# A decoder block on one core: modulation steps in pairs, work moved to ScalarE, and 18 matmuls of ones in the opening

## The chip, the cores and the metric

The kernel runs on 1 core of one Trainium2 chip. The metric is device time in microseconds, from the start to the end of one launch; less is better. The time before is the median of three runs. The profile shows one execution of the same program.

## The reference

One layer of a hybrid decoder block, 512 tokens of 1024 channels, all in float32:

```python
mod = silu(c) @ w_ada + b_ada            # c: (1, 1024), w_ada: (1024, 6 * 1024)
shift1, scale1, gate1, shift2, scale2, gate2 = split(mod, 6)
h = rms_norm(x, g_pre_mix) * (1 + scale1) + shift1
z = h @ w_in                             # GLU 2048 | q latent 384 | kv latent 256 | rotary key 64 | gates 2048
u = causal_depthwise_conv(ua * sigmoid(ub), 31 taps)
y_a = silu(layer_norm(u)) @ w_conv_out
y_b = mla_attention(...) @ w_attn_out    # 8 heads, rotary parts with cos and sin of the positions
x = x + gate1 * rms_norm((sigmoid(g_a) * y_a + sigmoid(g_b) * y_b) @ w_out, g_post_mix)
h = rms_norm(x, g_pre_mlp) * (1 + scale2) + shift2
x = x + gate2 * rms_norm(relu(h @ w_mlp_in) ** 2 @ w_mlp_out, g_post_mlp)
```

## The kernel before, in words

**Products.** A float32 product is made of three matmuls of a faster 32-bit type (`mm3`): each operand is split in a high part (a cast, on ScalarE) and a low part (the difference, on VectorE). So every weight block costs ScalarE one cast and VectorE one subtraction before TensorE can use it. TensorE transposes and the few products with ones remain in plain float32; one such product is recorded as two matmuls.

**Order of the work.** The function `emit` does not issue instructions. It records them, each with an engine, a cost and its dependences, in a `Planner`. The planner then simulates the five engines: TensorE takes of the ready operations the one with the lowest rank (its place in the program, less a `boost`), the others the one that is due first (`dead`, worked back from TensorE's schedule, less a `hurry`). It repeats this for up to `PASSES` = 14 allocations of the buffers, keeps the plan with the shortest simulated length and issues its order. Each engine's queue is thus a fixed order; on the chip semaphores alone delay it. `Planner.cost` holds the prices of instructions; the cost of a DMA's issue on SP is 375 ns there, a DMA's duration is worked out in `record`, and at most `DEPTH` = 8 loads are in flight on SP's queue. `plan.slack` adds a delay to the end of a POOL instruction in the simulation, `plan.after` a dependence on one operation. Both exist in the kernel before.

**The opening.** SP loads c (as `c8`, 8 rows of 128), x in four tiles, bias rows, and the first blocks of `w_ada`. TensorE transposes `c8` into a bank of PSUM (`bc`), VectorE and ScalarE form silu(c) in `cT`. x's tiles are normalised and transposed, 32 transposes in all, into `xnT`. Then the modulation of the first sublayer is formed for each block `k` of 128 channels (k = 0 to 7):

- `ada_load(ks, step)` loads the columns of shift and scale for the blocks in `ks`, in pieces of `step` rows of blocks; `KGRP` gives the groups, before `(1,)` to `(7,)`. One block's row in memory is 128 floats, 512 bytes.
- `ada_sums` multiplies by c: for k = 0 and 1 with TensorE (8 products of a column of `cT` by 128 x 256, 16 records each), for the others with VectorE (one `tensor_scalar` and seven `scalar_tensor_tensor` over 256 columns).
- `to_columns` sums over partitions with a product by ones, four small products for each k, and VectorE adds the bias and forms shift and scale (`mod[:, 0]`, `mod[:, 1]`).
- `first_products` forms h for block k from these (two activations and a difference) and multiplies seven blocks of `w_in` with it, 21 matmuls of 512 columns for each k, accumulating in seven banks of PSUM.

**After it** come the rest of the input projection, the latents, the rotary tables (`rp`: two Sin activations on ScalarE after the range reduction), attention by heads, the gates, the layer norm, the output products and the MLP. The convolution's 31 taps run on VectorE for eight channel blocks, spread over the products by `pump`: the first tap is a `tensor_scalar` that writes `cacc` from `upad`, the other 30 are `scalar_tensor_tensor`. They must be done before the layer norm, whose reciprocal root is a power on POOL (`lns`), followed by products of ones with a scaled identity that spread it over the partitions.

Nearly all instructions go through `record` and `issue`, so the profile gives them line 433; they are told apart by engine, tiles and shapes.

Of the kernel before, what the change touches and what calls it, by code (L numbers as in the profile page):

```python
# [17 lines left out]
P = 128  # L18
T = 512
# [36 lines left out]
ADAS = (1, 1, 0, 4)  # L56
KGRP = ((1,), (2,), (3,), (4,), (5,), (6,), (7,))
HL, SQ = 5e3, False
EXCL = True
LAG, AJ = 3000.0, 1  # L60
KOUT, VK = False, (0,)
ADD, LATE5 = 2.6, 1
HX, HA, HG, HC = 1.2e5, 1e5, 3e3, 1.1e5

# [114 lines left out]
class Planner:  # L179
# [68 lines left out]
    def cost(self, eng, fn, outs, ins, k):  # L248

        n = max(self.free_size(o) for o in (ins if fn == "reduce_sum" else outs))  # L250
        if fn == "dma_start":
            return (1200.0, 3000.0) if eng == "pool" else (375.0, 2000.0)
        psum = any(r.tensor.name.startswith("psum") for r in ins + outs)
# [7 lines left out]
        if eng == "act":  # L261
            t = 0.833 * n + (51 if psum else 93) + 93 * scalars + (900 if AF.Sin in self.args else 0)
            if fn == "activation" and any(isinstance(v, bass.AP) for v in outs[1:]):
                t += 93
            return t, 150.0
# [10 lines left out]
    def record(self, eng, fn, a, k):  # L276
# [19 lines left out]
        if fn == "dma_start":  # L296
            b = 4
            for _, c in outs[0].ap:
                b *= c
            n = min(self.run(outs[0]), self.run(ins[0]), 4096)  # L300
            o.dma = b * (6.0 + 0.040 * n) / (16 * n) * (ADD if eng == "pool" else 1)
        deps = set()
# [135 lines left out]
def tile_hybrid_block(  # L438
# [25 lines left out]
    def tile_of(shape, dtype, name):  # L464
        if name not in tiles:
            tiles[name] = const.tile(shape, dtype, name=name)
        return tiles[name]

    hD = [tc.dram_tile([P, KD * T], F32, name=f"h_spill{i}") for i in range(2)]
    yD = [tc.dram_tile([P, D], F32, name=f"y_spill{t}") for t in range(NT)]  # L470
    ident = const.tile([P, P], F32, name="ident")
    make_identity(nc, ident)
    ones = const.tile([P, P], F32, name="ones")
    nc.gpsimd.memset(ones, 1.0)
    nhalf = const.tile([P, 8], F32, name="nhalf")
# [11 lines left out]
    def emit(past, replay):  # L487
# [128 lines left out]
        plan.hurry = 0.0  # L616

        bc = pb.alloc()
        pe.transpose(pb.v(bc)[:, 0:8], c8, ident[:8, :8])
        cT = tile_of([P, 8], F32, "cT")  # L620
        tmp8 = tile_of([P, 8], F32, "tmp8")
# [20 lines left out]
        b1p = tile_of([P, 16], F32, "b1p")  # L642
        pool.tensor_scalar(b1p[:, 0:8], col("bada", 8, 8), 1.0, None, ALU.add)
        pool.tensor_scalar(b1p[:, 8:16], col("bada", 32, 8), 1.0, None, ALU.add)

# [36 lines left out]
        def to_columns(srcs, ks):  # L682

            for s in range(2):
                for i, k in enumerate(ks):
                    for src, lp in srcs:
                        pe.matmul(pb.v(bg)[:, s * KD + k:s * KD + k + 1], lhsT=src[:, s, i * P:(i + 1) * P],
                                  rhs=ones[0:lp, 0:1], start=src is srcs[0][0], stop=src is srcs[-1][0])
            ksl = slice(ks[0], ks[-1] + 1)
            dve.tensor_tensor(mod[:, 0, ksl], pb.v(bg)[:, ksl], col("bada", ks[0], len(ks)), ALU.add)  # L690
            for k in ks:
                dve.scalar_tensor_tensor(mod[:, 1, k:k + 1], pb.v(bg)[:, KD + k:KD + k + 1], b1p[:, k:k + 1], col("gpm", k),
                                         op0=ALU.add, op1=ALU.mult)

# [60 lines left out]

        for ks in KGRP:
            plan.hurry = HA - 1e4 * ks[0]
            ada = ada_load(ks, 1 if ks[0] == 1 and PE1 else KD // 2)
            ada_end = len(plan.ops) - 1
            plan.hurry -= 5e3  # L760
            wbs = [g1_load(k) for k in ks]
            plan.hurry = HG
            plan.boost = 1000
            if ks[0] == 1:
                plan.hurry = H1
                ada_sums(ks, ada, PE1, CH1)
            else:
                ada_sums(ks, ada)
            for k, wb in zip(ks, wbs):
                first_products(k, wb)  # L770
# [42 lines left out]
        rp = tile_of([P, 4, NT, NR], F32, "rp")  # L813
        ang, nn_, cosk, sink = (rp[:, i] for i in range(4))
        pool.tensor_tensor(ang, posT[:, :, None].broadcast_to([P, NT, NR]), invf[:, None, :].broadcast_to([P, NT, NR]), ALU.mult)
# [13 lines left out]
        dve.tensor_scalar(ngf, ngf, -1.0, float(np.float32(np.pi / 2)), ALU.mult, ALU.add)  # L829
        act.activation(sink, ang, AF.Sin)  # L830
        act.activation(cosk, nn_, AF.Sin)

# [18 lines left out]
        def conv_ops():  # L851
            for g in CONV_DVE:
                for kk in range(TAPS):
                    for ct in g:
                        if kk == 0:
                            cacc[ct] = fa.alloc(T)
                            dve.tensor_scalar(fa.v(cacc[ct]), fa.v(upad[ct])[:, 0:T], cw[:, ct, 0:1], col("cb", ct),
                                              ALU.mult, ALU.add)
                        else:
# [443 lines left out]
        def layer_norm():  # L1303
# [12 lines left out]
            dve.tensor_tensor(nb, ns, dm, ALU.subtract)  # L1316
            dve.tensor_tensor(va, va, rs, ALU.subtract)
            pool.tensor_tensor(rs, va, nhalf[:, :NT], ALU.pow)
            dve.tensor_tensor(nb, nb, rs, ALU.mult)

# [543 lines left out]
```

## Time and profile before

| | before |
|---|---|
| median of three runs | 808.56 us (807.07 to 809.38) |
| the profiled execution | 807.76 us, span 805.6 us, mean granted clock 0.998 |
| busy: TensorE / weight loads | 789.3 us (98%) / 687.6 us (85%) |
| busy: VectorE / ScalarE / POOL | 735.8 us (91%) / 476.6 us (59%) / 59.6 us (7%) |
| DMA | 130.99 MB, mean 163 GB/s |

Times in the profile count from the first instruction (span). The 2.2 us between span and time lie outside of it. An engine's busy share says where it works, not whether anyone waits for it; matmuls are pipelined, so a matmul's own duration (392 ns for 512 columns) is longer than the distance between two of them.

### The profile page before, as it was taken

Reading aid. Unit: us, or ns where it says so; the run is one execution under the profiler, and the core shown is the slowest. Engines: PE = TensorE matmul, PEld = TensorE weight load, DVE = VectorE, ACT = ScalarE, POOL = GpSimd, SP = SyncE. Lnnn points to the kernel's source line nnn. Section 1 sums busy time; section 2 is a strip of 40 time slices with the busy share of each in tenths; the row PEclk is TensorE's granted clock in tenths of the full one; section 3 lists DMA queues with packets and bytes.
Section 4 is the critical chain, followed back from the end, with each engine's and each line's share of the span. In section 5 each row is a group of like instructions: output and inputs, shape, how many; then the busy total and the mean of one; then the engine's idle time right before and its main releaser. Section 6 shows DMA issues by size and latency. Waiting matters only on the chain.

```text
span 805.6 us, 12015 instructions
## 1 busy us (share of the span) xinstructions
PE 789.3 (98%) x4450; PEld 687.6 (85%) x4450; DVE 735.8 (91%) x1052; ACT 476.6 (59%) x790; POOL 59.6 (7%) x121
## 2 busy tenths in 40 slices
PE   6999999999999999999999999999999999999996
PEld 3888988889897888878888889988998899889985
DVE  2899999999999999999898579899989978997998
ACT  5564463375886247238343268777667766777852
POOL 2001010000000000010000010001003300320023
PEclk9999999999999999999999999999999999999999
DMA  8999433010363272143997026149806940895176
GB/s 265 315 266 371 131 116 113 27 54 27 118 197 105 79 224 64 53 157 131 326 364 250 28 93 226 49 131 302 324 28 148 285 143 27 177 270 193 29 160 139
DMA packets 100364, 130.99 MB, mean 163 GB/s; under 512 B 8817, under 2 KB 67538, under 8 KB 100306
## 3 DMA queue, kind: packets, MB, share of 16 engines
q1 hardware_dynamic: 93970, 118.69, 44.7%
q0 software_dynamic: 6336, 11.54, 9.0%
q8 instruction: 35, 0.57, 0.3%
q14 instruction: 23, 0.19, 0.1%
HBM read 109.23 MB, written 20.97 MB: 162 GB/s over the span
## 4 chain that ended last, share of the span: by engine, by line
PE 84%; DVE 11%; issue 2%; ACT 2%; DMA 1%; POOL 0%; SPq 0%; DVEq 0%; ACTq 0%
PE psum L433 84%; DVE f_arena L433 6%; DVE r_arena L433 5%; ACT r_arena L433 1%; DMA rows<-in_b_ada_dram 1%; ACT f_arena L433 1%; DMA r_arena<-h_spill 0%; SPq L433 0%; POOL lns L433 0%; DVEq L1859 0%; POOL stats L433 0%; DVE lns L433 0%; DVE stats L433 0%; DVEq L433 0%; ACTq L433 0%
## 5 line engine op out<-in xcount | busy, mean ns | idle before, releaser
L433 PE MATMUL psum<-r_arena 128*128 128x512 f32 (+3 forms) x4108 | 749.4, 343 | 0.3 <-DVE r_arena L433 0.2
L433 PEld LDWEIGHTS psum<-r_arena 128*128 128x128 f32 x4108 | 647.8, 189 | 86.0 <-DVE r_arena L433 2.0
L433 ACT CAST r_arena<-f_arena 128x1024 fp32r<-128x1024 f32 (+4 forms) x249 | 236.6, 970 | 174.9 <-PE psum L433 115.2
L433 DVE TENSOR_TENSOR r_arena<-f_arena,r_arena 128x1024 fp32r<-128x1024 f32 (+5 forms) x259 | 278.0, 1101 | 26.5 <-ACT r_arena L433 23.7
L433 DVE SCALAR_TENSOR_TENSOR f_arena<-f_arena,cw 128x512 f32<-128x512 f32 x240 | 166.4, 754 | 0.0
L433 DVE TENSOR_TENSOR f_arena<-f_arena 128x1024 f32<-128x1024 f32 (+3 forms) x104 | 110.1, 1072 | 3.7 <-DMA f_arena<-in_w_mlp_in_dram 3.2
L433 ACT COPY f_arena<-psum 128x512 f32<-128x512 f32 (+4 forms) x107 | 57.5, 551 | 34.4 <-PE psum L433 30.4
L433 ACT ACTIVATE f_arena<-f_arena 128x512 f32<-128x512 f32 (+3 forms) x117 | 67.0, 593 | 17.2 <-DVE f_arena L433 16.2
L433 DVE SCALAR_TENSOR_TENSOR f_arena<-f_arena,cT 128x256 f32<-128x256 f32 (+1 forms) x70 | 54.4, 803 | 2.0 <-DMA f_arena<-in_w_ada_dram 1.6
L433 POOL DMA_DIRECT2D y_spill<-f_arena x40 | 34.8, 870 | 263.8 <-ACT f_arena L433 260.6
L433 DVE TENSOR_TENSOR f_arena<-psum,f_arena 128x512 f32<-128x512 f32 (+1 forms) x43 | 28.7, 677 | 12.1 <-PE psum L433 9.3
L433 PE MATMUL psum<-ident,f_arena 128*128 128x128 f32 x234 | 33.0, 280 | 5.2 <-DVE f_arena L433 5.2
L433 ACT ACTIVATE f_arena<-psum 128x512 f32<-128x512 f32 x35 | 20.5, 596 | 28.4 <-PE psum L433 21.2
L433 PEld LDWEIGHTS psum<-ident,f_arena 128*128 128x128 f32 x234 | 27.3, 143 | 11.0 <-DVE f_arena L433 5.5
L433 DVE TENSOR_TENSOR r_arena<-psum,r_arena 128x512 fp32r<-128x512 f32 (+2 forms) x57 | 36.0, 662 | 0.4
L433 ACT CAST r_arena<-psum 128x512 fp32r<-128x512 f32 (+2 forms) x57 | 30.0, 564 | 9.3 <-PE psum L433 8.9
L433 POOL TENSOR_TENSOR stats<-stats,nhalf 128x1 f32<-128x1 f32 (+1 forms) x17 | 12.3, 722 | 169.5 <-ACT stats L433 147.5
L433 ACT ACTIVATE r_arena<-f_arena 128x512 fp32r<-128x512 f32 (+3 forms) x21 | 13.5, 645 | 16.1 <-DVE f_arena L433 13.8
L433 ACT ACTIVATE r_arena<-psum 128x512 fp32r<-128x512 f32 x12 | 7.2, 598 | 24.5 <-PE psum L433 24.5
L433 POOL TENSOR_TENSOR lns<-lns,nhalf 128x4 f32<-128x4 f32 x1 | 2.0, 2046 | 251.4 <-DVE lns L433 251.4
L433 DVE CUSTOM_DVE_ANT_0 f_arena<-psum,mask 128x128 f32<-128x128 f32 (+3 forms) x32 | 15.0, 489 | 0.0
L433 DVE SCALAR_TENSOR_TENSOR f_arena<-f_arena 128x512 f32<-128x512 f32 (+1 forms) x18 | 13.3, 757 | 0.1
(94 smaller groups left out, 211.8 us busy)
## 6 DMA issues: line engine op xcount, KB each, us to landing
f_arena<-in_w_ada_dram SPq DMA_DIRECT2D x32, 512.0 KB, 5.0
f_arena<-in_w_mlp_in_dram SPq DMA_DIRECT2D x32, 512.0 KB, 9.4
f_arena<-in_w_mlp_out_dram SPq DMA_DIRECT2D x32, 512.0 KB, 5.7
f_arena<-in_w_in_dram SPq DMA_DIRECT2D x24, 512.0 KB, 4.4
y_spill<-f_arena POOLq DMA_DIRECT2D x40, 256.0 KB, 6.3
f_arena<-in_w_ada_dram SPq DMA_DIRECT2D x24, 256.0 KB, 5.9
f_arena<-in_x_dram SPq DMA_DIRECT2D x8, 512.0 KB, 7.4
h_spill<-r_arena SPq DMA_DIRECT2D x16, 256.0 KB, 6.6
```

The source lines that it names most:

```text
L433: getattr(self.real[o.eng], o.fn)(*o.a, **o.k)
```

## The change

Modulation blocks 2 to 7 are loaded and summed in pairs, so that a row in memory has 256 floats and VectorE's operations have 512 columns; the pieces loaded are two row blocks instead of four. The two steps that add bias and form scale go from VectorE to ScalarE, with a product b1g formed on POOL ahead of them. The convolution's first tap goes from VectorE to ScalarE. Sine and cosine are one activation over both halves of `rp`, whose order is changed for it. TensorE multiplies `ones` by `ones` three times before the transpose of c and fifteen times after it, into a bank that nothing reads, and `ones` is set ahead of the identity. The planner's numbers for a DMA's issue on SP, a DMA's duration and a Sin change, and the power of the layer norm gets 1100 ns of slack in the simulation. Since the order comes from the simulation, all queues may change their order.

```diff
-KGRP = ((1,), (2,), (3,), (4,), (5,), (6,), (7,))
+KGRP = ((1,), (2, 3), (4, 5), (6, 7))
...
+ISS = 480.0
+SPIN = (3, 15)
...
-            return (1200.0, 3000.0) if eng == "pool" else (375.0, 2000.0)
+            return (1200.0, 3000.0) if eng == "pool" else (ISS, 2000.0)
...
-            t = 0.833 * n + (51 if psum else 93) + 93 * scalars + (900 if AF.Sin in self.args else 0)
+            t = 0.833 * n + (51 if psum else 93) + 93 * scalars + (2566 if AF.Sin in self.args else 0)
...
-            o.dma = b * (6.0 + 0.040 * n) / (16 * n) * (ADD if eng == "pool" else 1)
+            o.dma = b * (6.0 + 0.043 * n) / (16 * n) * (ADD if eng == "pool" else 1)
...
+    ones = const.tile([P, P], F32, name="ones")
+    nc.gpsimd.memset(ones, 1.0)
     ident = const.tile([P, P], F32, name="ident")
     make_identity(nc, ident)
-    ones = const.tile([P, P], F32, name="ones")
-    nc.gpsimd.memset(ones, 1.0)
...
+        bw = pb.alloc()
         bc = pb.alloc()
+        def spin(n):
+            for _ in range(n):
+                pe.matmul(pb.v(bw)[:, 0:P], lhsT=ones, rhs=ones, start=True, stop=True)
+        spin(SPIN[0])
         pe.transpose(pb.v(bc)[:, 0:8], c8, ident[:8, :8])
+        plan.after = len(plan.ops) - 1
+        spin(SPIN[1])
+        plan.after = None
+        pb.free(bw)
...
+        b1g = tile_of([P, 8], F32, "b1g")
+        pool.tensor_tensor(b1g, b1p[:, 0:8], col("gpm", 0, 8), ALU.mult)
...
-            ksl = slice(ks[0], ks[-1] + 1)
-            dve.tensor_tensor(mod[:, 0, ksl], pb.v(bg)[:, ksl], col("bada", ks[0], len(ks)), ALU.add)
             for k in ks:
-                dve.scalar_tensor_tensor(mod[:, 1, k:k + 1], pb.v(bg)[:, KD + k:KD + k + 1], b1p[:, k:k + 1], col("gpm", k),
-                                         op0=ALU.add, op1=ALU.mult)
+                act.activation(mod[:, 0, k:k + 1], pb.v(bg)[:, k:k + 1], AF.Identity, bias=col("bada", k))
+                act.activation(mod[:, 1, k:k + 1], pb.v(bg)[:, KD + k:KD + k + 1], AF.Identity, scale=col("gpm", k),
+                               bias=b1g[:, k:k + 1])
...
-            ada = ada_load(ks, 1 if ks[0] == 1 and PE1 else KD // 2)
+            ada = ada_load(ks, 1 if ks[0] == 1 and PE1 else 2)
...
-        ang, nn_, cosk, sink = (rp[:, i] for i in range(4))
+        ang, nn_, sink, cosk = (rp[:, i] for i in range(4))
...
-        act.activation(sink, ang, AF.Sin)
-        act.activation(cosk, nn_, AF.Sin)
+        act.activation(rp[:, 2:4], rp[:, 0:2], AF.Sin)
...
-                            dve.tensor_scalar(fa.v(cacc[ct]), fa.v(upad[ct])[:, 0:T], cw[:, ct, 0:1], col("cb", ct),
-                                              ALU.mult, ALU.add)
+                            act.activation(fa.v(cacc[ct]), fa.v(upad[ct])[:, 0:T], AF.Identity, scale=cw[:, ct, 0:1],
+                                           bias=col("cb", ct))
...
+            plan.slack = 1100.0
             pool.tensor_tensor(rs, va, nhalf[:, :NT], ALU.pow)
+            plan.slack = 0.0
```

## The prediction

> **What bounds the kernel now.** I read the page first, its busy shares.
>
> ```profile
> span 805.6 us, 12015 instructions
> PE 789.3 (98%) x4450; PEld 687.6 (85%) x4450; DVE 735.8 (91%) x1052; ACT 476.6 (59%) x790; POOL 59.6 (7%) x121
> ```
>
> TensorE is busy for 98% of the span, so a microsecond taken from another engine is worth nothing unless TensorE waited for it. The next question is where the 16.3 us lie in which TensorE is not busy. The table by windows, cut at the stages, answers it (columns: window, length, busy time and instructions of PE, PEld, DVE, ACT, POOL, clock, DMA share, GB/s):
>
> ```profile
> 0.00:10.60 10.60, 2.90 (x12) 2.01 (x13) 2.56 (x7) 7.07 (x14) 4.62 (x47) 1.00 0.77 262
> 10.60:22.40 11.80, 11.80 (x59) 5.70 (x59) 3.59 (x7) 6.34 (x13) 1.21 (x3) 1.00 0.95 277
> 22.40:64.80 42.40, 42.40 (x200) 34.47 (x198) 39.07 (x87) 25.12 (x37) 0.68 (x6) 1.00 1.01 295
> 64.80:797.50 732.70, 731.91 (x4184) 645.37 (x4184) 685.86 (x945) 437.28 (x728) 51.78 (x65) 1.00 0.50 152
> 797.50:805.60 8.10, 0.29 (x3) 0.09 (x1) 4.70 (x11) 0.81 (x3) 1.35 (x2) 0.78 0.59 168
> ```
>
> 7.7 us of the idle time lie before 10.6, 7.8 in the tail after 797.5, and only 0.79 in the 733 us between. From 10.6 on the end is set by how fast TensorE works. The timeline of the opening shows that it does not work at full speed at first, whatever the clock column says:
>
> ```profile
> 1.27 0.20 POOL L474 MEMSET ones<- 128x128 f32 x1
> 2.35 0.24 PE L433 MATMUL psum<-ident,c 8*128 8x8 f32 x1 [2.35 <-DMA c<-in_c_dram]
> 7.80 1.76 PE L433 MATMUL psum<-ident,f_arena 128*128 128x128 f32 x7 [5.21 <-DVE f_arena L433]
> 9.69 0.18 PEld L433 LDWEIGHTS psum<-ident,rows 56*128 56x128 f32 x1 [0.54 <-DMA rows<-in_b_ada_dram]
> 10.60 5.07 PE L433 MATMUL psum<-f_arena,cT 128*1 128x256 f32 x16
> 10.98 0.13 PEld L433 LDWEIGHTS psum<-f_arena,cT 128*1 128x1 f32 x1 [0.30 <-issue]
> 11.41 0.13 PEld L433 LDWEIGHTS psum<-f_arena,cT 128*1 128x1 f32 x1 [0.30 <-issue]
> 13.54 1.62 PEld L433 LDWEIGHTS psum<-f_arena,cT 128*1 128x1 f32 x8 [0.30 <-issue]
> 17.63 3.61 PE L433 MATMUL psum<-f_arena,cT 128*1 128x256 f32 x16
> 22.46 2.32 PE L433 MATMUL psum<-r_arena 128*128 128x512 f32 x9
> ```
>
> The 16 records of the modulation's k = 0 come 0.43 us apart (10.98, 11.41) up to 13.54; from there eight take 1.62 us, 0.20 each. The same 16 records for k = 1 take 3.61 us instead of 5.07. TensorE ran at half speed until 13.5, 5.7 us after its first long burst and 2.9 us after the first record at 10.60.
>
> **The change, part by part.**
>
> *18 matmuls of ones.* A 128x256 float32 product is two records, so a 128x128 one costs half of 2 x 0.43 cold, 0.43 us, or 0.22 warm. `ones` is now set first on POOL, so three can start near 1.0 and end near 2.3, when the transpose of c starts anyway. The other 15 fill the gap to 7.80. Together, 18 x 0.43 = 7.7 us is more than the 5.7 us that the switch took at most. If the switch falls 2.9 to 5.7 us after 1.0, that is at 3.9 to 6.7, the rest runs at 0.22 and the spin ends at 6.5 to 7.9; with no switch at all at 2.6 + 15 x 0.43 = 9.0. It costs nothing in the first case, since TensorE waits for normalised x until 7.80, and at most 1.2 us in the other. What it brings: k = 0 takes 5.07 - 3.61 = 1.46 us less, and the start at 10.60, which hangs on the bias rows at 9.69 and a short cold transpose, comes about 0.4 earlier. The DMAs allow no more:
>
> ```profile
> 4.18 6.66 SPq L433 DMA_DIRECT2D f_arena<-in_w_ada_dram  x8
> 11.87 4.03 SPq L433 DMA_DIRECT2D f_arena<-in_w_ada_dram  x8
> 21.48 2.47 SPq L433 DMA_DIRECT2D f_arena<-in_w_ada_dram  x4
> f_arena<-in_w_ada_dram SPq DMA_DIRECT2D x16, 128.0 KB, 2.9
> f_arena<-in_w_ada_dram SPq DMA_DIRECT2D x24, 256.0 KB, 5.9
> 25.00:30.00 5.00, 5.00 (x26) 4.24 (x27) 4.29 (x12) 2.36 (x3) 0.31 (x3) 1.00 1.16 316
> 65.00:70.00 5.00, 5.00 (x23) 3.85 (x23) 3.66 (x10) 1.21 (x3) 2.74 (x8) 1.00 1.10 353
> L433 PE MATMUL psum<-r_arena 128*128 128x512 f32 x2182 | 510.9, 392 | 0.3 <-DVE r_arena L433 0.2
> 360.35 0.84 PE L433 MATMUL psum<-f_arena,ones 128*128 128x128 f32 x5 [0.34 <-DVE f_arena L433]
> ```
>
> The eighth load is issued near 10.4 and lands 2.9 later, at 13.3; with its 0.43 of matmul k = 0 can end at 13.7 instead of 15.67. For k = 1 the last lands near 18.3 and the work would end at about 19.3, so the gain is kept and first products start near 20.6 instead of 22.46. I take **-1.9 us**; the ends are 0 (no switch) and -2.9 (transposes move up as well).
>
> [...]
>
> *Modulation steps in pairs.* Each pair loads 1 KB rows in 8 DMAs in place of 512-byte rows in twice 4: as many DMAs and bytes on SP's queue. TensorE's column matmuls stay as many; what VectorE saves follows below. The price is that k = 2 waits for the loads of k = 3. Before, k = 2's first product comes after 42 products of 510.9 / 2182 = 0.234 us from 22.46 on and eight small column products (1.0, since five like them take 0.84 at 360.35), near 33.3; with the gain above it is wanted near 31.4. The loads of k = 3, the last issued near 23.1, landed near 23.1 + 5.9 = 29.0, behind the 128 x 896 floats of w_in for k = 2 (0.46 MB), which now come after: 1.45 us less at 316 GB/s, and 0.7 less if 1 KB rows move 2.1 MB at 353, as in 65 to 70, instead of 316. So the pair lands between 26.9 and 29.0. What remains of the chain is priced by these rows, which also carry the next part:
>
> ```profile
> L433 DVE TENSOR_TENSOR mod<-psum,cols x8: 154/156/159, 17.1 to 56.8; 128x1 f32<-128x1 f32 x8
> L433 DVE SCALAR_TENSOR_TENSOR mod<-psum,b1p,cols x8: 206/210/214, 17.2 to 56.9; 128x1 f32<-128x1 f32 x8
> L433 ACT ACTIVATE stats<-stats,epsc 128x1 f32<-128x1 f32 x16 | 4.4, 294 | 0.3
> L433 DVE TENSOR_SCALAR f_arena<-f_arena,cw,cols 128x512 f32<-128x512 f32 x8 | 4.4, 553 | 0.0
> L433 ACT ACTIVATE f_arena<-f_arena,lnh 128x512 f32<-128x512 f32 x16 | 12.2, 813 | 1.4 <-DVE f_arena L433 1.3
> L433 DVE SCALAR_TENSOR_TENSOR f_arena<-f_arena,cw 128x512 f32<-128x512 f32 x240 | 166.4, 754 | 0.0
> L433 DVE SCALAR_TENSOR_TENSOR f_arena<-f_arena,cT 128x256 f32<-128x256 f32 x42 | 18.7, 481 | 0.3
> 73.57 1.28 ACT L433 ACT_TABLE_LOAD   x1 [1.58 <-DVE rp L433]
> 74.86 0.31 ACT L433 ACTIVATE rp<-rp 128x128 f32<-128x128 f32 x1
> ```
>
> After the landing come two sums of 512 columns (2 x 0.754, the tap's form), the columns (1.0), two steps on ScalarE (2 x 0.294) and h (0.8): ready at 30.8 to 32.9. That is 0.6 early to 1.5 late, and up to 3.6 late if VectorE first does an h difference and a weight's (0.754, and 896/512 of it). I take **+0.3**; the ends are -0.5 (DMA time saved helps later) and +3.6. VectorE's sums fall from at most 16 x 0.481 = 7.7 us per pair to 0.55 + 7 x 0.754 = 5.8, so by up to 5.6 us for three pairs.
>
> *Mod steps and first conv tap on ScalarE, one sine.* VectorE loses 8 x (0.16 + 0.21) = 2.9 and 8 x 0.553 = 4.4 us; ScalarE gains 16 x 0.294 + 8 x 0.813 = 11.2, where it is idle 41% of the time. The mod step becomes 0.22 longer per k, behind nothing but ScalarE's own casts; the first tap waits for VectorE's `upad` and VectorE's second tap for it, with other taps between. One sine instruction of 256 columns for two of 128 (0.31 each) saves ScalarE under 0.3 us near 75: nothing, TensorE's work there covers it. POOL's extra 128x8 product is of the kind that already follows the columns: nothing.
>
> So VectorE is freed of up to 5.6 + 2.9 + 4.4 = 12.9 us, all before the layer norm. That counts only where TensorE stood still for it. The waits of TensorE's weight queue bound that:
>
> ```profile
> PEld psum L433 <- DVE f_arena L433: 6.7, 4, 5.3
> PEld psum L433 <- ACT f_arena L433: 2.5, 11, 0.3
> PEld psum L433 <- DVE r_arena L433: 2.0, 7, 0.6
> PEld psum L433 <- ACT r_arena L433: 0.9, 4, 0.3
> 357.93 2.05 POOL L433 TENSOR_TENSOR lns<-lns,nhalf 128x4 f32<-128x4 f32 x1 [251.39 <-DVE lns L433]
> ```
>
> Without the 5.3 us of the start these are 6.8 us, partly hidden behind running matmuls. A smaller part is VectorE's.
>
> *The planner's numbers.* The power step of the layer norm took 2.05 us, and TensorE stood 0.34 us (360.35) for what follows; 1.1 us of slack lets it put other matmuls there. The SP issue of 480 ns, the DMA rate and the Sin cost only reorder. For this and the freed VectorE I take **-1.0 us** of the 6.8; the ends are -3 (nearly half of the waits) and +2 (a new order with as many waits again as a third of these).
>
> **Sum.** -1.9 + 0.3 - 1.0 = -2.6 on the profiled execution's 807.76: 805.2 (span 805.6 to 803.0). The median of the three runs is 808.56, 0.8 higher; I forecast 805.3.
>
> **Rivals.**
> *The first pair comes late* (slower). If the landing is at its late end and VectorE's order puts two differences ahead of the sums, TensorE waits 3.6 us at k = 2, and half of it again at (4,5) and (6,7), where the same order would repeat, makes it 7.2 us: 807.76 + 7.2 - 1.9 - 1.0 is 812.1. For it: DMA share is 1.01 from 22.4 to 64.8. Against it: TensorE needs 42 x 0.234 + 1.0 = 10.8 us for a pair, DMA for 2.1 + 0.9 MB at 316 to 353 some 8.5 to 9.5, so lateness shrinks. It decides from 5.3 us of waiting on, 2.4 beyond the gains.
> *The clock gain is lost or spent* (no change). Either the clock is slow again when k = 0 starts, or k = 2 waits as long as the gain: 807.76 - 1.0 + 0.3 = 807.1. For the first: between the spin's end and 10.3 only transposes run, and in the rows above 1.76 us of them did not bring the switch. Against: the gap is 2.4 to 3.8 us, and the tail's clock of 0.78 shows the clock falling only after the last matmul. [...]
> *The new order also removes waits* (faster by more). VectorE with 12.9 us of air gives back 3 of the 6.8 us and the transposes of x move up: -2.9 - 3 + 0 gives 801.9.
>
> **How the numbers follow.** Forecast, gain 2.4 to 4.5 us: 0.43. More than that: 0.10. Gain lost or spent, within 2.4 us: 0.34, of which the slow clock is 0.07. First pair late and slower: 0.13. About 0.3%, 2.4 us, is what can be told from no change, and the forecast lies just beyond it, so faster is 0.53, same 0.34, slower 0.13. The range 802.2 to 808.6 leaves out the extreme of the faster case and most of the slower one; the forecast's own range is 803.3 to 805.4.
>
> **What would show it.** The 16 records of k = 0 in about 3.6 us, with no 0.43 spacing after 8 us; first 128x512 product near 20.6; sums of 128x512 in VectorE's rows, 21 of 0.754; TensorE busy without a break from 20.6 to 65; VectorE's total near 723 us; last matmul near 795. Wrong would be: k = 0's records still 0.43 apart, a gap of over 1 us on TensorE between 28 and 34, or TensorE waits above 7 us after 65.

## The result, and the profile after

The changed kernel takes 806.47 us (median of 20 runs, 805.52 to 807.20), the kernel before 808.53 (20 runs, 807.07 to 811.55). The ratio is 0.9973, with a 95% interval of 0.9966 to 0.998: faster by 2.2 us (the interval is 1.6 to 2.7 us, the medians differ by 2.1), against a forecast of 805.3. The profiled execution took 805.65 us, 0.8 below its median, as the one before was.

The page's head after the change, and the table by windows, cut as before but for 20.6 in place of 22.4, where the first products were expected (window, length, busy time and instructions of PE, PEld, DVE, ACT, POOL, then clock, DMA share, GB/s):

```profile
span 803.9 us, 12077 instructions
PE 793.3 (99%) x4486; PEld 693.1 (86%) x4486; DVE 728.7 (91%) x1004; ACT 483.7 (60%) x813; POOL 61.5 (8%) x122
0.00:10.60 10.60, 9.40 (x52) 8.28 (x53) 2.97 (x7) 7.24 (x15) 5.24 (x49) 1.00 0.81 273
10.60:20.60 10.00, 10.00 (x57) 5.02 (x54) 2.55 (x4) 6.58 (x14) 0.80 (x3) 1.00 0.91 262
20.60:64.80 44.20, 43.87 (x204) 35.27 (x203) 36.76 (x51) 28.67 (x50) 1.30 (x8) 1.00 1.00 326
64.80:797.50 732.70, 730.00 (x4180) 644.54 (x4178) 683.55 (x938) 441.19 (x735) 53.15 (x62) 1.00 0.50 150
```

TensorE is busy 4.0 us longer than before, and the kernel is shorter all the same: the first window now has 9.40 us of TensorE instead of 2.90, and 36 records of that are products of ones that nobody reads. Busy time of filler isn't progress. The timeline of TensorE's opening and of the end of the first products shows the progress:

```profile
1.00 1.65 PE L435 MATMUL psum<-ones 128*128 128x128 f32 x6 [1.00 <-POOL ones L474]
2.78 5.44 PE L435 MATMUL psum<-ones 128*128 128x128 f32 x30
8.06 0.93 PE L435 MATMUL psum<-ident,f_arena 128*128 128x128 f32 x7
9.86 2.75 PE L435 MATMUL psum<-f_arena,cT 128*1 128x256 f32 x12
12.80 1.02 PE L435 MATMUL psum<-f_arena,cT 128*1 128x256 f32 x4
15.89 3.61 PE L435 MATMUL psum<-f_arena,cT 128*1 128x256 f32 x16
21.08 8.57 PE L435 MATMUL psum<-r_arena 128*128 128x512 f32 x36
32.51 7.10 PE L435 MATMUL psum<-r_arena 128*128 128x512 f32 x30 [0.19 <-ACT r_arena L435]
63.44 0.25 PE L435 MATMUL psum<-ident,rows 37*128 37x37 f32 x1
```

Seven transposes that took 1.76 us before take 0.93, and the first 12 records of k = 0 take 2.75 us, 0.23 each: TensorE is at full speed when the transposes begin. k = 0 ends at 13.82 instead of 15.67. The last row is the transpose of the second set of bias rows, which follows the 168 first products (8 blocks of 21) in every version below; it came at 64.79 before. I use three such marks from here on: the start of the first product of 512 columns, of this transpose, and of the last matmul.

| kernel | first product | bias rows | last matmul | bias rows to last |
|---|---|---|---|---|
| before | 22.46 | 64.79 | 797.51 | 732.7 |
| after | 21.08 | 63.44 | 795.83 | 732.4 |

Of the 1.74 us by which the span fell (805.62 to 803.88), 1.35 are there when the first products end, 0.33 come in the 732 us behind them, and 0.06 in the tail (8.11 to 8.05 us after the last matmul starts). The remaining 0.37 of the profiled executions' 2.11 lie outside the span (2.14 to 1.77 us), where no row shows a cause.

The groups of the changed operations, and the waits of TensorE's weight queue (total, number, longest):

```profile
L435 DVE SCALAR_TENSOR_TENSOR f_arena<-f_arena,cT 128x512 f32<-128x512 f32 x21 | 15.8, 750 | 0.5
L435 ACT ACTIVATE mod<-psum,cols x8: 260/262/268, 15.2 to 50.2; 128x1 f32<-128x1 f32 x8
L435 ACT ACTIVATE mod<-psum,b1g,cols x8: 344/349/361, 15.4 to 50.4; 128x1 f32<-128x1 f32 x8
PEld psum L435 <- ACT f_arena L435: 2.4, 9, 0.7
PEld psum L435 <- DVE f_arena L435: 2.1, 4, 0.7
PEld psum L435 <- ACT r_arena L435: 2.1, 5, 0.8
PEld psum L435 <- DVE r_arena L435: 1.1, 6, 0.3
```

The wait of 5.3 us at the start is gone (filler stands there), but the others sum to 7.7 us, where they were 6.8 before. VectorE is busy 7.1 us less, and in sum TensorE does not wait less: more of the waits are behind ScalarE (4.5 us instead of 3.4), which took the work over. The same view from 65 us on shows where they lie: 5.4 us there (2.1, 0.7, 1.5 and 1.1 in the order above) instead of 6.3 (2.5, 1.4, 0.6 and 1.8), so the rise is all in the first 65 us, from 0.5 to 2.3.

### The profile page after: what moved, and what is told of

It reads as the page before. It is cut to its first block, busy times and chain, and to the rows that moved or that the text cites. A ratio compares the mean times of both kernels' runs of the same rounds, so it can differ in the third digit from the quotient of the medians.

```text
span 803.9 us, 12077 instructions
## 1 busy us (share of the span) xinstructions
PE 793.3 (99%) x4486; PEld 693.1 (86%) x4486; DVE 728.7 (91%) x1004; ACT 483.7 (60%) x813; POOL 61.5 (8%) x122
## 4 chain that ended last, share of the span: by engine, by line
PE 78%; DVE 15%; issue 2%; ACT 2%; DMA 1%; SPq 1%; POOL 0%; DVEq 0%; POOLq 0%; ACTq 0%
PE psum L435 78%; DVE f_arena L435 9%; DVE r_arena L435 6%; SPq L435 1%; ACT r_arena L435 1%; DMA f_arena<-in_x_dram 1%; ACT f_arena L435 1%; DMA f_arena<-in_w_ada_dram 1%; POOL stats L435 0%; DVEq L1875 0%; POOLq L1875 0%; ACT mod L435 0%; ACT stats L435 0%; DVE stats L435 0%; DVEq L435 0%
## 5 line engine op out<-in xcount | busy, mean ns | idle before, releaser
L435 DVE SCALAR_TENSOR_TENSOR f_arena<-f_arena,cw 128x512 f32<-128x512 f32 x240 | 164.5, 743 | 0.0
L435 DVE SCALAR_TENSOR_TENSOR f_arena<-f_arena,cT 128x1024 f32<-128x1024 f32 (+1 forms) x49 | 51.2, 1052 | 2.3 <-DMA f_arena<-in_w_ada_dram 1.7
L435 ACT ACTIVATE f_arena<-psum 128x512 f32<-128x512 f32 x35 | 20.6, 595 | 30.3 <-PE psum L435 30.3
L435 POOL TENSOR_TENSOR stats<-stats,nhalf 128x1 f32<-128x1 f32 (+1 forms) x17 | 14.1, 828 | 165.6 <-ACT stats L435 139.9
```

Source lines behind the costliest of these rows:

```text
L435: getattr(self.real[o.eng], o.fn)(*o.a, **o.k)
```

## The experiments

Theory: the gain is the clock's, kept because the pairs and the freed VectorE let the first products and what follows run earlier. Rivals: the clock alone makes it; or the new order alone does, and the filler is idle play. In the spins' removal (a2, f1) and in g1 the order of the changed kernel is kept, and in a1 that of the kernel before; all others are planned anew, so an edit also moves other work. Each profile is of one execution, and executions of one program differ by 1.5 us and more; small differences of a mark are read together with the median.

| run | first product | bias rows | last matmul | bias rows to last | median, and ratio to before |
|---|---|---|---|---|---|
| a1_spins_alone | 21.05 | 64.47 | 798.07 | 733.6 | 808.43, 1.0007 (0.9996 to 1.0018) |
| d1_spins_planned | 20.91 | 64.53 | 799.97 | 735.4 | 810.22, 1.0027 (1.0015 to 1.0039) |
| b1_numbers_alone | 24.83 | 67.01 | 798.92 | 731.9 | 807.91, 0.9990 (0.9980 to 1.0001) |
| a2_spins_out | 23.26 | 65.27 | 797.74 | 732.5 | 807.55, 0.9996 (0.9987 to 1.0005) |
| a3_single_steps | 21.56 | 64.85 | 797.88 | 733.0 | 808.30, 0.9999 (0.9990 to 1.0009) |
| a4_on_vector | 21.29 | 63.65 | 797.22 | 733.6 | 807.43, 0.9995 (0.9986 to 1.0004) |
| e1_tap_on_vector | 21.30 | 63.56 | 795.88 | 732.3 | 807.57, 0.9989 (0.9980 to 0.9998) |
| b3_pairs_late | 24.39 | 66.51 | 799.39 | 732.9 | 808.59, 0.9991 (0.9979 to 1.0003) |
| f1_eight_spins | 26.02 | 68.01 | 800.45 | 732.4 | 808.68, 0.9997 (0.9986 to 1.0008) |
| g1_rows_earlier | 21.71 | 63.92 | 796.53 | 732.6 | 806.21, 0.9976 (0.9964 to 0.9989) |
| c1_half_loads | 21.79 | 64.36 | 796.07 | 731.7 | one run, 805.78 |
| c2_half_sums | 22.21 | 63.82 | 796.18 | 732.4 | one run, 806.19 |

**The spins alone, in the order of before.**

```diff
+        # issue(): 3 before TensorE's first operation, 15 after it; ones is set ahead of ident
+        nc.tensor.matmul(PT[:, 7, 0:P], lhsT=ones, rhs=ones, start=True, stop=True)
```

> The kernel before, every queue in its old order, with the 18 matmuls of ones put around the transpose of c (into PSUM bank 7) and the ones set first; nothing else of the change. Theory one (the gain is the clock in the opening): the 16 records of k = 0 take 3.6 us instead of 5.07, the last matmul comes 1.7 us earlier (about 795.8), time 1.5 to 2.0 us below before, ratio 0.9975 to 0.998. Theory two (the gain comes from the work taken off VectorE and the new order): the old order waits for VectorE's results anyway, so what the opening wins is lost again on TensorE before 250 us, and the ratio is 0.999 to 1.001.

The timeline of the opening, and one place far behind it:

```profile
10.09 3.61 PE L436 MATMUL psum<-f_arena,cT 128*1 128x256 f32 x16
21.05 0.95 PE L436 MATMUL psum<-r_arena 128*128 128x512 f32 x3
21.09 0.94 ACT L436 CAST r_arena<-f_arena 128x896 fp32r<-128x896 f32 x1 [2.68 <-DMA f_arena<-in_w_in_dram]
21.93 2.26 ACT L436 COPY f_arena<-psum 128x512 f32<-128x512 f32 x5
22.56 0.19 PEld L436 LDWEIGHTS psum<-r_arena 128*128 128x128 f32 x1 [1.01 <-ACT f_arena L436]
628.88 1.23 DVE L436 TENSOR_TENSOR f_arena<-f_arena 128x1024 f32<-128x1024 f32 x1 [2.24 <-DMA f_arena<-in_w_mlp_in_dram]
631.30 3.02 PE L436 MATMUL psum<-r_arena 128*128 128x512 f32 x12 [0.78 <-DVE r_arena L436]
```

The clock does come (k = 0 in 3.61 us), and the first product starts 1.4 us earlier than before. But ScalarE's queue holds a cast ahead of its copies out of PSUM, and the cast waited 2.68 us for a weight that landed at 21.09 (the same cast started at 21.02 in the kernel before). So TensorE waits 1.01 us, the bias rows come only 0.3 us earlier, and a late MLP load takes even that in this execution. The median does not move. Three of the 11 runs (809.81 to 811.64) have a mean clock of 0.992 to 0.996; the median of the eight others, 808.3, is that of the kernel before, 808.34, as well. The clock alone is worth nothing in the old order.

**The same, planned.** Would a plan that knows of the spins keep the gain?

```diff
+        ...                # the change's block with SPIN = (3, 15), in the kernel before; ones is set ahead of ident
+        spin(SPIN[0])
         pe.transpose(pb.v(bc)[:, 0:8], c8, ident[:8, :8])
+        plan.after = len(plan.ops) - 1
+        spin(SPIN[1])
+        plan.after = None
```

> The kernel before with the 18 matmuls recorded in the planner, so that it may order all queues around them; pairs, mod steps, taps and numbers as before. Theory (after the first four runs): VectorE cannot feed TensorE 1.5 us earlier with steps of one block, whatever the order, so first products start near 21 and the last of the 168 still ends at 64.5 to 65.1; ratio 0.9985 to 1.0005. Rival: only the old order stood in the way (ScalarE's copies behind a cast), and with a new one the 168th product comes near 63.5 and the ratio is 0.998 or less.

No; it is slower, by more than either theory allowed. Five of its 11 runs also show a lower mean clock (0.993 to 0.995), but the six others, 808.75 to 810.22, lie above the kernel before (808.38) as well. The bias rows come at 64.53, no better than in the fixed order, and the new plan has a wait of its own right behind them (timeline of TensorE):

```profile
64.53 0.25 PE L434 MATMUL psum<-ident,rows 37*128 37x37 f32 x1
66.41 0.96 PE L434 MATMUL psum<-r_arena 128*128 128x512 f32 x3 [1.63 <-ACT f_arena L434]
```

**The planner's numbers alone.**

```diff
-            return (1200.0, 3000.0) if eng == "pool" else (375.0, 2000.0)
+            return (1200.0, 3000.0) if eng == "pool" else (480.0, 2000.0)
...
+            plan.slack = 1100.0     # at the layer norm's power; Sin 2566 and 0.043 as in the change
```

> The kernel before with only the planner's numbers of the change (SP issue 480, DMA rate 0.043, Sin 2566, 1100 of slack on the layer norm's power), planned anew. Theory: the numbers only reorder; TensorE's wait at the layer norm (0.66 us above the usual distance between 340 and 360) goes, others stay, ratio 0.999 to 1.0005. Rival: a new order alone is worth the whole gain, ratio 0.998 or less.

From the bias rows to the last matmul it needs 731.9 us, 0.8 less than before, and TensorE's wait in front of the layer norm's 16 products of ones is gone. In this execution, without filler, TensorE's opening is slower than before (73 records take 16.59 us up to 24.8, where 71 took 14.70 up to 22.4), which hides the gain in the profile; in the median it is 0.1%, with an interval that touches no change.

**The spins taken out of the change.**

```diff
+            if o.eng == "pe" and "lhsT" in o.k and o.k["lhsT"] is o.k["rhs"]:
+                continue            # issue(): the order stays, the 18 products are not issued
```

> The changed kernel, every queue in its order, with only the 18 matmuls of ones left out when the instructions are issued. Theory one: half clock until 13 us comes back, k = 0's 16 records cost 1.5 us more, last matmul 1.7 us later, ratio to before 0.9995 to 1.0005 and above. Theory two: the freed VectorE lets TensorE catch up, ratio stays near 0.9975.

TensorE's timeline has k = 0 cold again; it ends at 16.00, 2.2 us later than with the filler, and the last matmul comes 1.9 us later where 1.7 was expected:

```profile
7.88 1.76 PE L437 MATMUL psum<-ident,f_arena 128*128 128x128 f32 x7 [5.28 <-DVE f_arena L437]
10.69 4.11 PE L437 MATMUL psum<-f_arena,cT 128*1 128x256 f32 x12
14.98 1.02 PE L437 MATMUL psum<-f_arena,cT 128*1 128x256 f32 x4
65.27 0.25 PE L437 MATMUL psum<-ident,rows 37*128 37x37 f32 x1
```

With the order held the same, the filler is worth 1.83 us at the bias rows (65.27 against 63.44), 1.9 in the last matmul, and 0.0023 of the time, 1.9 us, in the medians' ratios. The order alone (0.9996) brings nothing that can be told. Neither rival stands.

**Single steps instead of pairs, the rest as in the change.**

```diff
-KGRP = ((1,), (2, 3), (4, 5), (6, 7))
+KGRP = ((1,), (2,), (3,), (4,), (5,), (6,), (7,))
```

> The changed kernel with the modulation steps one by one again (groups of one block, pieces of four row blocks), planned anew. Theory one, with the pairs a small cost: the two waits of TensorE between 30 and 33 us (0.4 and 0.2 us) go, the products end 0.3 to 0.6 us earlier, ratio 0.9965 to 0.997. Theory two: VectorE gets up to 5.6 us of work back and the ratio rises to 0.998 to 0.999. A new plan alone may move either by some tenths of a us.

The whole gain goes, more than either theory expected, although the first product comes at 21.56, 0.9 us ahead of that of the kernel before. Of the 2.05 us by which the last matmul comes later than in the change, 0.5 are there at the first product, 0.9 come between it and the bias rows, and 0.6 behind them. All queues were planned anew, and only the 0.9 are followed here. The windows from 40 to 60, of the changed kernel and of this one, show them:

```profile
40.00:60.00 20.00, 19.99 (x94) 16.42 (x94) 17.71 (x26) 15.42 (x27) 0.25 (x2) 1.00 0.89 287
40.00:60.00 20.00, 19.13 (x89) 14.97 (x88) 19.28 (x37) 14.96 (x26) 0.25 (x2) 1.00 0.95 273
```

VectorE is busy 19.28 of 20 us, TensorE stands still for 0.87 and fits in 89 records instead of 94. DMA, at 0.95, is busy too. Two runs try to separate them; both keep single steps.

That this is the steps and not one unlucky plan, the marks of the other versions show. From the first product to the bias rows it takes 43.3, 43.4 and 43.6 us with filler and single steps (a3, a1, d1), three different orders; 42.2 to 42.4 with filler and pairs (the change, a4, e1, g1); and 42.0 to 42.3 with either where no filler brought the clock, so that the first product came late (the kernel before, b1, a2, f1).

**Half of the loads, and half of the sums, for k from 2 on.**

```diff
-            for j in range(0, KD, step):
+            for j in range(0, KD if ks[0] < 2 else KD // 2, step):     # c1, ada_load; the sums read the half twice
...
+                if ks[0] >= 2 and j >= KD // 2:                        # c2, ada_sums: VectorE's last four left out
+                    continue
```

> Single steps in the changed kernel, with half of the modulation's loads for k = 2 to 7 left out; VectorE makes all its sums, over the first half of the rows twice, so the result is not the reference's. If DMA is what holds single steps back, the waits of TensorE between 40 and 60 us (2.0 us in the run with single steps) fall below 0.6 and the 168th product comes near 63.5. If VectorE is, they stay above 1.3 and it comes at 64.5 or later.

> Single steps in the changed kernel with all loads, and VectorE's sums for k = 2 to 7 over half of the rows only (four operations of 256 columns instead of eight), so the result is not the reference's. If VectorE is what holds single steps back, TensorE's waits between 40 and 60 us fall below 0.6 and the 168th product comes near 63.5; if the bytes are, it comes at 64.5 or later.

The same window, first with half of the loads, then with half of the sums:

```profile
40.00:60.00 20.00, 20.00 (x95) 16.58 (x94) 17.96 (x35) 14.81 (x26) 0.37 (x3) 1.00 0.68 205
40.00:60.00 20.00, 20.00 (x93) 16.59 (x92) 12.30 (x20) 11.99 (x19) 0.25 (x2) 1.00 0.92 265
```

Either one fills TensorE in this window. With half of the sums the first products and the bias rows lie 41.6 us apart, with half of the loads 42.6, with neither 43.3. The difference between the two runs is one wait outside the window, in the timelines of TensorE and ScalarE with half of the loads:

```profile
33.11 0.96 PE L435 MATMUL psum<-r_arena 128*128 128x512 f32 x3 [0.95 <-ACT r_arena L435]
30.86 0.95 ACT L435 CAST r_arena<-f_arena 128x896 fp32r<-128x896 f32 x1 [2.04 <-DMA f_arena<-in_w_in_dram]
```

ScalarE stood 2.04 us for a block of w_in, with the two steps and h of k = 2 behind that cast in its queue, and TensorE then waited 0.95 us for h. So both limits were near and relief on either side is enough. Which of them counts for more is not shown: with fewer loads VectorE's busy time falls too (19.28 to 17.96 us in the window), the bias rows of c1 (64.36) lie between what the two theories expected, and each run is one execution of a new order.

**Modulation steps and tap back on VectorE; then the tap alone.**

```diff
-                            act.activation(fa.v(cacc[ct]), fa.v(upad[ct])[:, 0:T], AF.Identity, scale=cw[:, ct, 0:1],
-                                           bias=col("cb", ct))
+                            dve.tensor_scalar(fa.v(cacc[ct]), fa.v(upad[ct])[:, 0:T], cw[:, ct, 0:1], col("cb", ct),
+                                              ALU.mult, ALU.add)     # e1; a4 also has the two steps on mod as before
```

> The changed kernel with the mod steps and the first conv tap on VectorE again, planned anew. Theory one (TensorE does not wait for VectorE's 7.3 us): same as the changed kernel within 0.5 us, ratio 0.997 to 0.998. Theory two: TensorE's waits between 150 and 260 us grow by 1 us or more, ratio 0.998 to 0.9995.

> The changed kernel with only the first conv tap on VectorE again, planned anew; the mod steps stay on ScalarE. The run with both on VectorE had TensorE 1.2 us later between the 168th first product and the end, most of it at the layer norm. If the taps carry that (4.4 us of VectorE work after 69 us), TensorE's waits between 340 and 360 us are again near 1.2 us and the ratio is 0.9985 to 0.9995. If the mod steps or a chance of the new order do, they stay near 0.1 us and the ratio is 0.997 to 0.998.

In a4 the opening is that of the change (63.65), and 1.2 us are lost behind it, most of them at the layer norm and not between 150 and 260 as expected. TensorE's timeline there, of the change, of a4 and of e1:

```profile
359.31 1.95 PE L435 MATMUL psum<-f_arena,ones 128*128 128x128 f32 x16
358.71 2.02 PE L435 MATMUL psum<-f_arena,ones 128*128 128x128 f32 x16 [0.92 <-issue]
359.09 1.95 PE L435 MATMUL psum<-f_arena,ones 128*128 128x128 f32 x16
```

With the tap alone on VectorE the layer norm has no wait, and the last matmul starts at 795.88, as in the change. Its profiled run took 806.0, but its median is 807.57, 0.0016 worse by the ratios, and the intervals just meet (0.998). So the trace gives the tap's move no value and the times allow it some; whether in a4 the steps themselves or only the other order brought the wait back stays open. So no run shows what the two moves to ScalarE are worth by themselves. That 1100 ns of slack do not by themselves keep the wait away, a4 shows.

**The first pair dissolved**, to price the wait for it.

```diff
-KGRP = ((1,), (2, 3), (4, 5), (6, 7))
+KGRP = ((1,), (2,), (3,), (4, 5), (6, 7))
```

> The changed kernel with steps 2 and 3 single and only 4 and 5, 6 and 7 as pairs. If the first pair's late landing costs TensorE its waits between 20 and 40 us (1.2 us, 0.6 of them at 32), these fall below 0.7, the 168th product comes near 62.6 and the ratio is 0.9965 to 0.997. If VectorE's time is what counts, 1.9 us more of sums make later blocks late instead: waits between 40 and 60 us above 0.8 and a ratio of 0.9975 or more.

First product to bias rows is 42.1 us, 0.2 less than in the change. That does not price the pair: a2 and f1 keep the pair and the change's order, have a late first product like this run, and need 42.0. What those two show is that the change's order needs up to 0.35 us less here when it starts 2.2 to 4.9 us later; the price of the first pair is at most a part of that. The time is no better, and the opening shows one reason. TensorE's timeline:

```profile
7.74 0.98 PE L435 MATMUL psum<-ident,f_arena 128*128 128x128 f32 x7 [0.29 <-DVE f_arena L435]
10.84 0.24 PE L435 MATMUL psum<-ident,rows 56*128 56x56 f32 x1 [2.11 <-DMA rows<-in_g_pre_mix_dram]
11.49 4.44 PE L435 MATMUL psum<-f_arena,cT 128*1 128x256 f32 x12
16.12 1.02 PE L435 MATMUL psum<-f_arena,cT 128*1 128x256 f32 x4
```

This is the rival of the slow clock. The seven transposes run at full speed (0.98), then TensorE waits 2.11 us for a small load, and 12 records of k = 0 take 4.44 us instead of 2.75. The window in which they stand 0.43 apart has a granted clock (third column from the end) of 0.50:

```profile
11.87:15.28 3.41, 3.41 (x9) 1.01 (x8) 0.88 (x2) 0.00 (x0) 1.13 (x4) 0.50 0.93 266
```

Between the filler's end near 7.5 and the fall at 11.87, 4.4 us, TensorE ran eleven transposes and the first two records of k = 0, and waited the 2.11 us. In the change, e1 and g1 eleven transposes lie there too, yet 12 records of k = 0 take 2.75 to 2.77 us. There it is 1.6, 2.6 and 3.0 us from the filler's end to k = 0 and no wait for a load is longer than 0.45; here it is 4.0. So the transposes alone did not bring the fall in those; whether the long wait did in b3 is not shown. Four of b3's 11 runs took 806.2 to 806.9 us, seven 807.8 to 809.95. 3.41 us at half speed is 0.002 of the span's mean clock, and the profiled run (809.12) has 0.996. The mean is a blunt measure, since the tail moves it also: behind the last matmul the clock is 0.78 in the profile of the kernel before and 0.67 in the change's, over 8.1 us, which takes 0.0022 and 0.0033 off the mean. Of the seven, three have 0.995 or 0.996 and four 0.997 or 0.998, like the quick ones. So the fallback explains some of them at most, and the value of this grouping stays open.

**Eight spins instead of 18.**

```diff
+        left = 8                     # issue(): the first eight of the 18 are issued, in the change's order
...
```

> The changed kernel, every queue in its order, with the first 8 of the 18 matmuls of ones issued and 10 left out: TensorE multiplies ones until about 5 us and waits until 8. If about 3.5 us of work bring the clock up and it stays up over a pause of 3 us, as with 18: k = 0's records at 0.22 us from the start, ratio 0.997 to 0.998. If the clock does not rise or falls back in the pause: 0.43 us spacing until about 13 us, 1.8 us later, ratio 0.999 to 1.0. [...]

TensorE's timeline of the opening:

```profile
2.77 2.50 PE L440 MATMUL psum<-ones 128*128 128x128 f32 x10
7.87 1.76 PE L440 MATMUL psum<-ident,f_arena 128*128 128x128 f32 x7 [2.59 <-DVE f_arena L440]
11.31 0.32 PE L440 MATMUL psum<-ident,rows 56*128 56x56 f32 x1 [1.69 <-DMA rows<-in_g_pre_mix_dram]
12.39 5.16 PE L440 MATMUL psum<-f_arena,cT 128*1 128x256 f32 x12
17.74 1.02 PE L440 MATMUL psum<-f_arena,cT 128*1 128x256 f32 x4
```

And the row of the table by windows that lies over k = 0:

```profile
12.39:17.30 4.91, 4.91 (x13) 1.34 (x12) 0.91 (x2) 0.00 (x0) 1.16 (x4) 1.00 0.86 255
```

In this execution filler from 1.0 to 5.3 us did not bring the clock: the transposes take 1.76 us again and k = 0 is cold to 17.3. The clock of that window still says 1.00: the column shows the fall from full speed (0.50 in b3) and not this slow start. That makes the mean clock of the other runs readable. The profiled one (810.27) and one more have 0.998, like the profiles in which the clock came up only in k = 0 (the kernel before, a2); the other nine have 0.993 to 0.997, eight of them at most 0.995, which is more than the tail takes. By b3's measure (0.002 for 3.41 us) 0.003 less is, by my estimate, some 5 us at half speed after a rise. So with eight products the clock seems to come in most executions and to be lost again, most likely ahead of k = 0; that is an estimate from the means, not seen in a trace. The change's 20 runs have 0.996 to 0.998. With 18 products the distance of the records falls from 0.21 to 0.11 us at 6.6 us in the change; in a1, b3 and e1 the 30 records behind the transpose of c took 5.90, 4.68 and 4.70 us, where 0.21 each would make 6.4. Of the two lengths only the longer one made the kernel faster (median 806.47 against 808.68); whether it is needed to lift the clock or to reach closer to the work is not shown. (The opening is also late here for the rows' load.)

**The bias rows' load earlier**, since b3 and f1 both waited for it.

```diff
+        rows = [o for o in order if o.eng == "sp" and o.k["out"].tensor.name.startswith("rows0")]
+        ...                # issue(): these two are issued on SP ahead of the third tile of x
```

> The changed kernel, every queue in its order but for one place: the two small loads of bias and g_pre_mix rows go ahead of the third tile of x on SP's queue instead of behind the fourth. In two runs TensorE waited 1.7 and 2.1 us for these rows, and in one of them the clock fell back to half. Theory (this wait and the clock that falls back in it are the opening's scatter): the rows are there before TensorE needs them near 8.8, k = 0 starts at 9.4 to 9.9, no second half-speed stretch, the slowest runs go, median 805.5 to 806.3, ratio 0.9965 to 0.9975. Rival: x's third and fourth tile come 1.1 us later by the two issues, transposes wait for them, ratio 0.998 to 0.999.

```profile
8.75 0.27 PE L438 MATMUL psum<-ident,rows 56*128 56x56 f32 x1
10.47 2.77 PE L438 MATMUL psum<-f_arena,cT 128*1 128x256 f32 x12 [0.38 <-DMA f_arena<-in_w_ada_dram]
11.33 0.09 PEld L438 LDWEIGHTS psum<-f_arena,cT 128*1 128x1 f32 x2 [0.35 <-DMA f_arena<-in_w_ada_dram]
```

The rows are there 0.4 us earlier and TensorE now waits for `w_ada` instead; k = 0 starts at 10.47, 0.6 later and not at 9.4 to 9.9 as expected. One of the nine runs still took 808.76. Its 0.9976 and the change's 0.9973 can't be told apart. No version beat the change.

## Why the prediction was right, point by point

**Direction and size.** The kernel got faster, and most of it in the opening (1.35 of the 1.74 us of span), as forecast. The size was two thirds of the forecast: 2.1 to 2.2 us instead of 3.3 (808.56 to 805.3). The range of 802.2 to 808.6 holds the result, but its upper end is the time before, so that alone says little; 806.47 lies outside the forecast's own 803.3 to 805.4. A gain of 2.4 to 4.5 us had the chance of 0.43; the measured one, just under 2.4, falls in the next case, 0.34, though neither of the causes given for that case occurred in the profile. A good half of the miss of 1.2 us is in the base of the sum: the 2.6 us were taken off the profiled execution's 807.76, and of the 0.8 by which the median was higher only 0.1 was added. From 808.56 the same terms give 806.0. The rest, 0.5, is in the terms.

**The first check.** It held: k = 0 runs at full speed, without the spacing of 0.43. The spin took until 8.2, a little past the 7.9 worked out for a switch by 6.7 (it came at 6.6), and the transposes behind it start at 8.06 instead of 7.80.

**The clock, -1.9.** Right in size: k = 0 ends 1.85 us earlier, and a2 gives 1.83 at the bias rows and 1.9 in the ratio. What I did not see is its condition. I priced it as a term that adds to the others; a1 and d1 show that it is worth nothing without the rest. The first product came at 21.08 and not 20.6, because k = 1 ended at 19.50 instead of 19.3 and the four column products of k = 1, 0.5 us, were put ahead of it in place of three of the twelve transposes that stood there before.

**The pairs, +0.3.** About right in size: between 20 and 40 us TensorE is idle for 0.32 us where it was not idle before, and the same order needs 0.35 less when it starts later (a2, f1). There was no gap over 1 us between 28 and 34 (the longest was 0.6 by the distance of the matmuls, near 32), so the rival of a late pair did not occur. But the sign was that of one end only. Against single steps at the new clock the pairs bring about 1 us between the first product and the bias rows (42.2 to 42.4 against 43.3 to 43.6), and the whole version 2.1 us by the ratio (a3), with a new order in it. The step that failed is the comparison: I costed the pairs against the old timing, where single steps fed TensorE, and booked VectorE's saving for waits in general, while TensorE, 1.9 us earlier, was about to outrun the sums and loads of k = 3 to 7. The step "k = 2 is wanted near 31.4" should have been asked of the old steps also.

**VectorE freed and the planner's numbers, -1.0.** Mis-sized: 0.33 us from the bias rows to the last matmul. I took 1.0 of 6.8 us of waits. Behind 65 us these fell by 0.9 (6.3 to 5.4, well under the 7 named as a sign of being wrong), but partly hidden waits are not time, and those of the first 65 us grew. The wait at the layer norm went (0.5 us between 340 and 380, from the distances of matmuls), and others grew near 200 and 460 by some 0.3 and 0.4. Nor can the gain be put down to VectorE: b1, with the planner's numbers alone, needs 731.9 us there, less than the change's 732.4.

VectorE fell by 7.1 us, to 728.7, not to 723. The removed and replaced operations did lose 12.4 us of their own time (the sums 5.1, the two steps 2.9, the taps 4.4), close to the 12.9 forecast. But VectorE's instructions overlap in the profile: their own times (mean times number, over all rows) add up to 819.2 us before and 799.0 after, 20.2 less, where the busy time fell by 7.1. I took the own time of an operation for what its removal frees. On ScalarE the two steps took 262 and 349 ns where I had 294, which mattered to nobody.

**Tail, 0.** Right: 8.11 to 8.05.

**Rivals.** The slow clock, which I gave 0.07, did not come in the profiled execution of the change but did in b3. The reason given, only transposes between the spin and k = 0, held in the change, e1 and g1 as well, where k = 0 ran at full speed; b3 had besides a wait of 2.11 us for a small load, which I had not given, and what brought the fall is not shown. That the new order removes waits (801.9) did not happen to that extent. In span, -1.6 was forecast for the opening and 1.35 measured; the rest of what is missing is the 0.7 of the VectorE term.

## What to carry to other kernels

When TensorE is 98% busy, take its waits and its speed stage by stage; an engine's freed microseconds count only where TensorE stood still for it, and an operation's own time is not yet a freed microsecond. Parts of a change are not terms of a sum: the versions without the filler, without the pairs and with the work back on VectorE lose 1.9, 2.1 and 1.8 us of a gain of 2.2. Only the first of these keeps every queue's order. The others carry a new order too, and a1 and d1, the same work in two orders, differ by 1.6 us (1.1 without the runs of low mean clock); so how much of the 2.1 and 1.8 is the part and how much the order stays open. For the pairs the stretch from the first product to the bias rows shows the part itself, about 1 us: a front that moves earlier keeps its lead only if each later supplier (loads, sums, casts in a fixed queue) can move with it. So price an added step against the new timing, and ask of the old step whether it could have kept up.

## What the runs showed of the hardware

- Filler and the clock: behind eight float32 products of 128 columns, from 1.0 to 5.3 us, the seven transposes of f1's profile took 1.76 us, as without filler, and eight of its 11 runs have a mean clock of 0.993 to 0.995. Behind 18, about 7 us, the seven took 0.93 to 0.99 us in the profiles of the change, a1, b3, e1 and g1; in the change the distance of the records halved at 6.6 us, 5.6 us after the first of them. In a1 three of 11 runs still show means of 0.996 or less and in d1 five of 11 means of 0.993 to 0.995.
- The granted clock's column is blind to the start: 1.00 over the cold 4.91 us of f1, and 0.50 over the 3.41 us of b3 in which the clock had been up and fell. The spacing of equal matmuls shows both (0.43 against 0.20 to 0.23 us).
- The small bias rows, loaded behind big blocks, landed so late in b3 and f1 that TensorE waited 2.11 and 1.69 us for them, and 0.20 in the changed kernel, which has the loads in f1's order. Whether executions of one program differ by this too is not shown, since each has one profile.
- VectorE's instructions overlap: their own times add up to 819.2 us in the kernel before, in a busy time of 735.8.
